# Seven products for the down projection, pair products in one bank, and the up projection's conv in PSUM

## The chip, the cores and the metric

The kernel runs on one core of a Trainium2 chip. The metric is the device time of one execution in microseconds; the time of a kernel is the median of its runs. Beside the timed runs one execution is profiled, and its span (first to last instruction) is a little shorter than its time.

## What is computed

One decoder layer on 1024 tokens of width 1024, all float32. Two mixers and an output projection come first; the change touches only what follows them, the gated feed-forward block:

```python
h = rms_norm(x, norm_ffn_g[i])
u = causal_depthwise_conv(h @ w_up[i], conv_ffn_w[i], conv_ffn_b[i])     # FFN_CONV = 3
u_gate, u_val = jnp.split(u, 2, axis=-1)                                 # D_FF = 2816 columns each
x = x + (jax.nn.silu(u_gate) * u_val) @ w_down[i]
```

## The kernel before

**Matmuls.** Each float32 operand is split into a rounded high part and the low rest (`split`, lines 151 to 154: ScalarE casts, another engine subtracts), and `mm3` (lines 173 to 177) makes one product of three matmuls: high by high, high by low, low by high. Each takes a 128x128 stationary tile and 512 moving columns and adds into one PSUM bank. There are eight banks: two in the pool `pl` (tile `lin`) and six in `psd` (tile `dps`, function `bank6`).

**Up projection.** The 2816 gate columns and as many value columns form 22 column tiles j of 128 each. One tile j covers gate tile j and value tile j for both halves of the tokens: a 2x2 block product, with the contraction of 1024 cut in two. It is made with seven products instead of eight, in the Winograd form of Strassen's method, each of 12 matmuls: p1 and p2 (`p12`), p3 (`22`), p4 (`t4`), p5 (`t1`), p6 (`t2`), p7 (`t3`). The activations' quarters and their sums (`BQ`) stay in SBUF for all j. The weights' sums are made for each j by GpSimd (`w_sums`), and their splits by `w_first`, `w_second` (GpSimd subtracts), `w_third`, `w_fourth` (VectorE subtracts).

Banks of one tile before: x holds p1 and then p1+p6; y holds p2, then p7+p4; z holds p5, then p5+p3. VectorE adds across banks: `c11` = y + a copy of x, `both_sums` q = z + s2 (s2 a copy of x), `c22` = y + q, p3's sum = z + s2, `c21` = y + s2. A matmul that adds to a bank waits until the reads of that bank are done.

`conv` then runs per kind on the whole row of 1024 tokens in an SBUF tile (`uc0`, `uc1`): ScalarE writes bias and last tap, VectorE adds two taps. `gate` applies silu on ScalarE; `value` multiplies on VectorE (line 1368) and stores the row to DRAM (`a_d`, line 1369).

**Order.** TensorE's instructions are chained in program order to the end. From `strict` to `strict_end` (tiles j = 0 and 1 with the activations' quarters made beside them) every engine but SP is chained too. Elsewhere the scheduler places each engine's instructions, earlier lines of the program first where several are ready, so work written later can be placed earlier. Tile j = 2 comes through the strict part with its p1 and p2 done, in two banks of `psd`. The loop `for j in range(3, FFT + 1)` computes tile j - 1 (`q`) while it prepares tile j (`nx`); its product order before is p5, p6, p7, p3, p4, then p12 of the next tile. In its last round `first_acts` loads the first four rows for the down projection.

**Down projection.** For each half of the output columns: eight banks (one for each 128 tokens), eleven pairs of 128-rows kp, each with 2 x 8 products of three matmuls. Weights are split by ScalarE and VectorE (`load_w`), and the rows of `a_d` are loaded and split once for each half. At the end VectorE adds the residual (`xr`) and SP stores.

Of the kernel before, what the change touches and what calls it, by code (L numbers as in the profile page):

```python
# [9 lines left out]
F32 = mybir.dt.float32  # L10
# [7 lines left out]
P = 128  # L18
# [54 lines left out]
def tile_hybrid_layer(ctx: ExitStack, tc: tile.TileContext, x, cols, cons, w_main, w_small, w_uq, w_ukv,  # L73
# [34 lines left out]
    def col(c):  # L108
        return cl[:, c:c + 1]
# [42 lines left out]
    def split(raw, hi, lo, eng=None):  # L152
        S.copy(hi, raw)  # L153
        (eng or V).tensor_sub(lo, raw, hi.bitcast(F32))  # L154
# [8 lines left out]
    def load_w(src, shape):  # L163
        hi = wpool.tile(shape, F32R, name="whi")
        lo = wpool.tile(shape, F32R, name="wlo")
        n = shape[1] // 2
        for j in range(2):
            s = slice(j * n, (j + 1) * n)
            flat = "p a b -> p (a b)"
            load_split(src[:, s, :].rearrange(flat), 512, hi[:, s, :].rearrange(flat), lo[:, s, :].rearrange(flat))  # L170
        return hi, lo

    def mm3(ps, a, b, first, last, **more):
        (ah, al), (bh, bl) = a, b
        PE.matmul(ps, lhsT=ah, rhs=bh, start=first, stop=False, **more)  # L175
        PE.matmul(ps, lhsT=ah, rhs=bl, start=False, stop=False, **more)  # L176
        PE.matmul(ps, lhsT=al, rhs=bh, start=False, stop=last, **more)  # L177
# [979 lines left out]
    def w_third(q):  # L1157
        q.c = w_split(q.r2, w_tiles(2), V)
# [4 lines left out]
    def bank6():  # L1163
        return psd.tile([P, 512], F32, name="dps")
# [5 lines left out]
    with tc.tile_pool(name="ep", bufs=2) as ep:  # L1170
# [117 lines left out]


        tp = tpctx.enter_context(tc.tile_pool(name="tp", bufs=12, side="right"))  # L1290
        a_d = dram.tile([FFT * P, T], F32, name="a_d")
# [19 lines left out]
        def c11(q):  # L1311
            s1 = lt.tile([P, 512], F32, name="lt")
            S.copy(s1, q.x)
            V.tensor_tensor(q.ug[:, 2:514], q.y, s1, op=ALU.add)

        def p5(q):
            q.z = bank6()
            drain([product(q.z, q.b, 0, "t1", True, True)])

        def p6(q, sums=True):  # L1320
            drain([product(q.x, q.b, 4, "t2", False, True)])
            q.s2 = lt.tile([P, 512], F32, name="lt")
            S.copy(q.s2, q.x)
            if sums:
                both_sums(q)

        def both_sums(q):
            q.q = lt.tile([P, 512], F32, name="lt")
            V.tensor_tensor(q.q, q.z, q.s2, op=ALU.add)
# [8 lines left out]

        def c22(q):
            value_row(q)  # L1340
            V.tensor_tensor(q.uv[:, 514:1026], q.y, q.q, op=ALU.add)

        def conv(q, kind, u):
            c = ux[0].tile([P, T], F32, name=f"uc{kind}", bufs=2 - kind)
            ct = kind * FFT + q.j
            cw = CG_FW + 3 * ct
            S.activation(c, u[:, 2:T + 2], AF.Identity, bias=col(CG_FB + ct), scale=col(cw + 2))
            for k in range(2):
                V.scalar_tensor_tensor(c, u[:, k:k + T], col(cw + k), c, op0=ALU.mult, op1=ALU.add)
            return c  # L1350

        def p3(q):
# [1 line left out]
            V.tensor_tensor(q.ug[:, 514:1026], q.z, q.s2, op=ALU.add)  # L1354

        def gate(q):
            q.gate = conv(q, 0, q.ug)
            S.activation(q.gate, q.gate, AF.Silu)

        def p4(q):  # L1360
            drain([product(q.y, q.e or q.c, 0 if q.e else 4, "t4", False, True)])

        def c21(q):
            V.tensor_tensor(q.uv[:, 2:514], q.y, q.s2, op=ALU.add)

        def value(q):
            c = conv(q, 1, q.uv)
            V.tensor_tensor(q.gate, q.gate, c, op=ALU.mult)
            nc.sync.dma_start(out=a_d[q.j * P:(q.j + 1) * P, :], in_=q.gate)

# [52 lines left out]
        low()  # L1423
        flush()
        for q in (q0, q1):
            p5(q)
        def sums(q):

            q.q = q.ug[:, 514:1026]
            V.tensor_tensor(q.q, q.z, q.s2, op=ALU.add)  # L1430
# [6 lines left out]
        p6(q0, False)  # L1437
        sums(q0)
# [3 lines left out]
        p6(q1, False)  # L1442
# [5 lines left out]
        V.tensor_tensor(q0.q, q0.y, q0.q, op=ALU.add)  # L1448
        sums(q1)
        for i in range(2):  # L1450
            job("22", i, b[4, i], act_tile())
        p7(q1)
        V.tensor_tensor(q1.q, q1.y, q1.q, op=ALU.add)
        for i in range(2, 4):
            job("22", i, b[4, i], act_tile())
        low()
# [19 lines left out]
    rows = "p a b -> p (a b)"  # L1476
    first = []

    def first_acts(k):
        raw = up.tile([P, KD, P], F32, name=f"ur{1 + k % 2}", bufs=2).rearrange(rows)  # L1480
        nc.sync.dma_start(out=raw, in_=a_d[k * P:(k + 1) * P, :])
        first.append([tp.tile([P, 2, 512], F32R, name="tq").rearrange(rows) for _ in range(2)])
        split(raw, *first[k])

    for j in range(3, FFT + 1):
        nx = None
        if j < FFT:
            nx = Pair()
            nx.j = j
            w_raw(nx)  # L1490
            w_first(nx)
        p5(q)
        if j == 3:
            gate_row(q)
            c11(q)
# [9 lines left out]
        if nx:  # L1505
            w_second(nx)
        if not nx:
            for k in range(2):
                first_acts(k)
        p7(q)  # L1510
        c22(q)
# [8 lines left out]
        if not nx:  # L1520
            for k in range(2, 4):
                first_acts(k)
        value(q)
        if nx:
            w_third(nx)
            drain([p12(nx)])
            c11(nx)
        q = nx


    upctx.close()

    with tc.tile_pool(name="fp", bufs=6) as fp:
        for ch in range(2):
            banks = [bank6() if t < 6 else lin_tile() for t in range(NT)]
            xrs = []
            for kp in range(FFT // 2):
                wh, wl = load_w(w_down[ch, kp], [P, 2, 512])
                if kp == FFT // 2 - 2:
                    for t in range(NT):  # L1540
                        xrs.append(fp.tile([P, 512], F32, name="xr", bufs=8))
                        nc.sync.dma_start(out=xrs[t], in_=x2_d[t * P:(t + 1) * P, ch * 512:(ch + 1) * 512])
                pair = []
                for k in range(2 * kp, 2 * kp + 2):
                    if ch == 0 and k < 4:
                        pair.append(first[k])
                        continue
                    ar = fp.tile([P, T], F32, name="ar")
                    nc.sync.dma_start(out=ar, in_=a_d[k * P:(k + 1) * P, :])
                    hi = hp.tile([P, T], F32R, name="h")  # L1550
                    lo = hp.tile([P, T], F32R, name="h")
                    split(ar, hi, lo)
                    pair.append((hi, lo))
                last = kp == FFT // 2 - 1
                order = [(k, t) for t in range(NT) for k in range(2)] if last else \
                    [(k, t) for k in range(2) for t in range(NT)]
                for k, t in order:
                    hi, lo = pair[k]
                    tk = slice(t * P, (t + 1) * P)
                    mm3(banks[t], (hi[:, tk], lo[:, tk]), (wh[:, k, :], wl[:, k, :]), kp == 0 and k == 0, last and k == 1)  # L1560
                    if last and k == 1:
                        V.tensor_tensor(xrs[t], banks[t], xrs[t], op=ALU.add)
                        nc.sync.dma_start(out=out[tk, ch * 512:(ch + 1) * 512], in_=xrs[t])
    tpctx.close()
    uctx.close()

# [92 lines left out]
```

## Time and profile before

| what | value |
|---|---|
| median of 3 runs | 2217.35 us (2217.06 to 2220.04) |
| profiled execution, its own time | 2218.69 us |
| its span | 2216.9 us |
| TensorE matmul busy | 2174.5 us (98%), 11104 matmuls recorded |
| VectorE (DVE), ScalarE (ACT), GpSimd (POOL) busy | 1426.3, 1006.5, 818.5 us |
| mean granted TensorE clock | 0.995 |

How to read the rows: "L1141" is line 1141 of the kernel, which may be a helper's. A row of a group reads: line, engine, operation, written tile <- read tiles, shapes, count, then busy time and the mean time of one (ns), then idle time of the engine just before them and what ended it. A row of a timeline reads: start, duration (both us), engine, line, operation, tiles, with the idle time before it in brackets. A row of waits reads: who <- on whom: total us, times, longest. A row of windows gives for each engine its busy time and the instructions that touch the window. Matmuls overlap each other, so their spacing is taken from counts per time, not from the duration of one.

### The profile page before, as it was taken

To read this page: it belongs to the slowest core of one execution; us is meant where nothing else is said; L and a number is where in the kernel's file an instruction comes from. 1 tells how busy PE (TensorE), PEld (TensorE's weight loads), DVE (VectorE), ACT (ScalarE), POOL (GpSimd) and SP (SyncE) were. 2 spreads that over 40 slices of the span, in tenths; PEclk is the share of its full clock that TensorE was granted. 3 is DMA by queue.
4 is the path that set the end of the run, shared out by engine and by line. 5 is a ranking of instruction groups with operands and counts; after the bars stand their busy time and mean duration, and the time that the engine had idled before them with its cause. 6 is when DMAs were issued, how large, how long until landed. Compare 5 with 4: busy or idle time off the path is not lost.

```text
span 2216.9 us, 30483 instructions
## 1 busy us (share of the span) xinstructions
PE 2174.5 (98%) x11104; PEld 1748.1 (79%) x11104; DVE 1426.3 (64%) x2480; ACT 1006.5 (45%) x1820; POOL 818.5 (37%) x911
## 2 busy tenths in 40 slices
PE   8999999999999999999999999999899999999999
PEld 6887777777777887878878788887688888888887
DVE  4566656675664469898786745546977777764432
ACT  5445454544453446666564424335544444443220
POOL 2234433442343247665546210012555555510000
PEclk9999999999999999999999999999899999999999
DMA  4221111101212224645276566542122222246631
GB/s 146 71 65 54 40 48 59 54 32 53 69 43 100 80 86 147 195 143 185 83 240 206 173 223 197 168 159 92 67 95 86 86 76 86 78 143 244 205 127 67
DMA packets 115751, 253.52 MB, mean 114 GB/s; under 512 B 13136, under 2 KB 25360, under 8 KB 115600
## 3 DMA queue, kind: packets, MB, share of 16 engines
q1 hardware_dynamic: 103104, 210.54, 28.5%
q0 software_dynamic: 11008, 37.76, 5.3%
q10 hardware_dynamic: 1488, 3.28, 0.4%
q8 instruction: 87, 1.43, 0.3%
q14 instruction: 64, 0.52, 0.1%
HBM read 194.63 MB, written 56.89 MB: 113 GB/s over the span
## 4 chain that ended last, share of the span: by engine, by line
PE 80%; DVE 9%; DMA 4%; ACT 4%; issue 2%; POOL 1%; SPq 0%; ACTq 0%; DVEq 0%; POOLq 0%
PE lin L175 13%; PE lin L177 13%; PE lin L176 13%; PE dps L176 8%; PE dps L175 8%; PE dps L177 8%; PE pv L670 2%; PE s L175 2%; PE s L176 2%; PE s L177 2%; PE s L627 1%; DMA wraw<-in_w_ssd 1%; PE yp L891 1%; PE sn L874 1%; PE s L610 1%
## 5 line engine op out<-in xcount | busy, mean ns | idle before, releaser
L175 PE MATMUL lin<-h,whi 128*128 128x512 f32 x1440 | 592.2, 411 | 0.3 <-DVE lt L330 0.3
L177 PE MATMUL lin<-h,wlo 128*128 128x512 f32 x1440 | 564.0, 392 | 0.0
L176 PE MATMUL lin<-h,whi 128*128 128x512 f32 x1440 | 562.9, 391 | 0.0
L175 PEld LDWEIGHTS lin<-h,whi 128*128 128x128 f32 x1440 | 271.0, 188 | 82.5 <-issue 33.6
L177 PEld LDWEIGHTS lin<-h,wlo 128*128 128x128 f32 x1440 | 270.8, 188 | 59.9 <-DVE wlo L154 0.2
L176 PEld LDWEIGHTS lin<-h,whi 128*128 128x128 f32 x1440 | 271.9, 189 | 52.9 <-issue 6.7
L153 ACT CAST whi<-wraw 128x512 fp32r<-128x512 f32 x276 | 166.0, 619 | 285.6 <-PE lin L176 115.6
L154 POOL TENSOR_TENSOR wlo<-wraw,whi 128x512 fp32r<-128x512 f32 x134 | 192.5, 1455 | 164.1 <-ACT whi L153 163.9
L664 POOL TENSOR_TENSOR acc<-acc,e 128x512 f32<-128x512 f32 (+3 forms) x80 | 78.7, 984 | 251.1 <-ACT e L659 227.6
L659 ACT ACTIVATE e<-s 128x512 f32<-128x512 f32 (+1 forms) x192 | 93.6, 493 | 169.0 <-DVE s L657 142.9
L154 DVE TENSOR_TENSOR wlo<-wraw,whi 128x512 fp32r<-128x512 f32 x142 | 97.0, 704 | 99.4 <-ACT whi L153 99.2
L154 DVE TENSOR_TENSOR h<-ar,h 128x1024 fp32r<-128x1024 f32 x40 | 48.7, 1225 | 109.2 <-ACT h L153 104.8
L850 ACT ACTIVATE seg<-abc,acum 128x128 f32<-128x128 f32 x256 | 80.2, 390 | 51.0 <-PE yp L891 45.0
L153 ACT CAST h<-ar 128x1024 fp32r<-128x1024 f32 x40 | 42.0, 1054 | 125.4 <-PE lin L176 114.1
L176 PE MATMUL dps<-wlo,h 128*128 128x512 f32 x240 | 93.4, 389 | 0.0
L175 PE MATMUL dps<-whi,h 128*128 128x512 f32 x240 | 93.4, 389 | 0.0
L177 PE MATMUL dps<-whi,h 128*128 128x512 f32 x240 | 93.4, 389 | 0.0
L812 DVE SCALAR_TENSOR_TENSOR xg<-craw,cl,xg 128x1024 f32<-128x1024 f32 x48 | 73.8, 1538 | 27.4 <-ACT xg L810 26.9
L664 DVE TENSOR_TENSOR acc<-acc,e 128x512 f32<-128x512 f32 (+3 forms) x80 | 55.0, 688 | 37.6 <-ACT e L659 37.0
L1140 ACT CAST xhi<-ur 128x512 fp32r<-128x512 f32 (+1 forms) x41 | 34.0, 830 | 90.3 <-PE dps L176 84.2
L670 PE MATMUL pv<-e,vt 128*64 128x512 f32 (+3 forms) x384 | 72.9, 498 | 0.0
L629 DVE CUSTOM_DVE_ANT_0 s<-s,negw 128x128 f32<-128x128 f32 (+3 forms) x128 | 62.3, 495 | 13.6 <-PE s L627 13.5
(587 smaller groups left out, 5045.8 us busy)
## 6 DMA issues: line engine op xcount, KB each, us to landing
wraw<-in_w_main SPq DMA_DIRECT2D x112, 256.0 KB
ur<-in_w_up SPq DMA_DIRECT2D x44, 512.0 KB
ar<-a_d SPq DMA_DIRECT2D x40, 512.0 KB
abc<-ac_d POOLq DMA_DIRECT2D x32, 512.0 KB, 5.2
wraw<-in_w_ssd SPq DMA_DIRECT2D x64, 256.0 KB
wraw<-in_w_down SPq DMA_DIRECT2D x44, 256.0 KB
a_d<-uc SPq DMA_DIRECT2D x22, 512.0 KB
g_d<-lt SPq DMA_DIRECT2D x32, 256.0 KB
```

Source lines behind the costliest of these rows:

```text
L153: S.copy(hi, raw)
L154: (eng or V).tensor_sub(lo, raw, hi.bitcast(F32))
L175: PE.matmul(ps, lhsT=ah, rhs=bh, start=first, stop=False, **more)
L176: PE.matmul(ps, lhsT=ah, rhs=bl, start=False, stop=False, **more)
L177: PE.matmul(ps, lhsT=al, rhs=bh, start=False, stop=last, **more)
L629: V.tensor_tensor_reduce(ps[:, 0:w], ps[:, 0:w], negw[:, 512 - w:512], 1.0, 2 * NEG, ALU.add, ALU.max, nm[:, j, i:i + 1])
L659: S.activation(e[:, c0:512], ps[:, 0:w], AF.Exp)
L664: (V if hd else G).tensor_tensor(accs[hd][:, c0:512], accs[hd][:, c0:512], e[:, c0:512], op=ALU.add)
L670: PE.matmul(pv[hd * 64:(hd + 1) * 64, c0:512], lhsT=vt[:, j, hd * 64:(hd + 1) * 64], rhs=es[hd][:, c0:512], start=first, stop=last)
L812: V.scalar_tensor_tensor(c, raw[:, k:k + T], col(cw + k), c, op0=ALU.mult, op1=ALU.add)
L850: S.activation(seg[:, hd, :], abc[:, hd, :], AF.Relu, bias=acum[:, c, 8 * g + hd:8 * g + hd + 1], scale=-1.0)
L1140: S.copy(hi, r)
```

## The change

Four things are done together.

1. *Down projection.* It becomes a 2x2 block product too: two halves of the tokens by two halves of the output columns, contracted over pairs of 128-rows (even rows, odd rows). Seven products replace eight. They run in four passes over the eleven pairs; the banks `xb` (four) and `yb` (four) collect them, and `evacuate` adds banks to result tiles between passes: pass 1 ends with xb and yb into `r11`, pass 2 with xb into `r12` and yb into `r22`, pass 3 with xb into `r22` and yb into `r12`, pass 4 (one product) with xb into `r21`.
2. *Operands for it.* `value` now makes, for each pair of tiles, the sums of gated quarters on GpSimd (one after the even tile, four after the odd) and stores seven quarters to `f_d`, three from SP and four from GpSimd's queue. The weights' sums are made on GpSimd within passes 2, 3 and 4. `first_operands` loads and splits operands and weights of the first four pairs in the last round.
3. *Pair products in one bank.* p7 and p4 add to x as p6 did, so x holds p1, p1+p6, p1+p6+p7, then p4 on top. `both_sums` goes; ScalarE copies z after p5 instead (q), `c22` = x + q, and `c21` is a ScalarE copy of x. The loop's order becomes p5, p6, p3, p7, p12 of the next tile, p4, and `w_third` follows p4. In the last round p4 has a bank of its own, q.y.
4. *Conv in banks.* `conv` works on half the tokens, with its result in a bank of `psd` (`bank6`) instead of SBUF; gate and value call it twice, and silu and the product read the bank.

```diff
-        def p5(q):
+        def p5(q, z=None):
             q.z = bank6()
             drain([product(q.z, q.b, 0, "t1", True, True)])
+            q.q = lt.tile([P, 512], F32, name="lt") if z is None else z
+            S.copy(q.q, q.z)

-        def p6(q, sums=True):
+        def p6(q):
             drain([product(q.x, q.b, 4, "t2", False, True)])
             q.s2 = lt.tile([P, 512], F32, name="lt")
             S.copy(q.s2, q.x)
-            if sums:
-                both_sums(q)
...
         def p7(q):
-            q.y = bank6()
-            drain([product(q.y, q.c, 0, "t3", True, True)])
+            drain([product(q.x, q.c, 0, "t3", False, True)])
...
-            V.tensor_tensor(q.uv[:, 514:1026], q.y, q.q, op=ALU.add)
+            V.tensor_tensor(q.uv[:, 514:1026], q.x, q.q, op=ALU.add)

-        def conv(q, kind, u):
-            c = ux[0].tile([P, T], F32, name=f"uc{kind}", bufs=2 - kind)
+        def conv(q, kind, u, half):
+            c = bank6()
...
+            n = half * 512
+            S.activation(c, u[:, n + 2:n + 514], AF.Identity, bias=col(CG_FB + ct), scale=col(cw + 2))
             for k in range(2):
-                V.scalar_tensor_tensor(c, u[:, k:k + T], col(cw + k), c, op0=ALU.mult, op1=ALU.add)
+                V.scalar_tensor_tensor(c, u[:, n + k:n + k + 512], col(cw + k), c, op0=ALU.mult, op1=ALU.add)
...
         def gate(q):
+            q.gate = ux[0].tile([P, T], F32, name="uc0", bufs=2)
+            for half in range(2):
+                S.activation(q.gate[:, hs_(half)], conv(q, 0, q.ug, half), AF.Silu)
...
         def c21(q):
-            V.tensor_tensor(q.uv[:, 2:514], q.y, q.s2, op=ALU.add)
+            S.copy(q.uv[:, 2:514], q.x)

         def value(q):
-            c = conv(q, 1, q.uv)
-            V.tensor_tensor(q.gate, q.gate, c, op=ALU.mult)
-            nc.sync.dma_start(out=a_d[q.j * P:(q.j + 1) * P, :], in_=q.gate)
+            for half in range(2):
+                g = q.gate[:, hs_(half)]
+                V.tensor_tensor(g, g, conv(q, 1, q.uv, half), op=ALU.mult)
+            kp = q.j // 2
+            t0, t1 = q.gate[:, 0:512], q.gate[:, 512:1024]
+            def total(n, a, b, op, t):
+                G.tensor_tensor(t, a, b, op=op)
+                if n:
+                    nc.gpsimd.dma_start(out=f_d[kp][:, n, :], in_=t)
+                return t
+            def raw():
+                return wpool.tile([P, 512], F32, name="wraw", bufs=2)
+            if q.j % 2 == 0:
+                nc.sync.dma_start(out=f_d[kp][:, 0, :], in_=t0)
+                even[:] = [t1, total(4, t1, t0, ALU.subtract, ux[0].tile([P, 512], F32, name="ud", bufs=1))]
+            else:
+                nc.sync.dma_start(out=f_d[kp][:, 1:7:5, :], in_=q.gate.rearrange("p (a b) -> p a b", b=512))
+                total(2, even[0], t1, ALU.add, raw())
+                total(3, even[1], t1, ALU.add, raw())
+                t = total(0, t1, t0, ALU.subtract, raw())
+                total(5, t, even[1], ALU.add, t)
```

The loop's new order, and the core of the down projection (pass 1, whose first four pairs come from `first`; pass 2; the end of pass 4):

```diff
         p5(q)
...
         p6(q)
...
         p3(q)
...
         gate(q)
         if nx:
             w_fourth(nx)
-        p4(q)
-        c21(q)
...
+        p7(q)
+        c22(q)
         if nx:
-            w_third(nx)
             drain([p12(nx)])
             c11(nx)
+            p4(q)
+            c21(q)
+            w_third(nx)
...
+        value(q)
...
+        for k in range(nk):
...
+            products(xb, halves(a, 0), bs[0], k == 0, False)
+            if k < 4:
+                others.append((halves(a, 1), bs[1]))
+                if k < 3:
+                    continue
+                for n in range(3):
+                    products(yb, *others[n], n == 0, False)
+            products(yb, halves(a, 1), bs[1], False, k == nk - 1)
+        evacuate(ALU.add, r11, xb, r11)
+        evacuate(ALU.add, r11, yb, r11)
+        stored(0, 0, r11)
+        for k in range(nk):
+            a = acts(k, 2)
+            w = raw_w()
+            nc.sync.dma_start(out=w, in_=w_down[1, k])
+            G.tensor_tensor(w[:, 0, :], kept[:, k, :], w[:, 0, :], op=ALU.subtract)
+            G.tensor_tensor(kept[:, k, :], w[:, 1, :], w[:, 0, :], op=ALU.add)
...
+            products(xb, halves(a, 1), bs[0], False, False)
+            products(yb, halves(a, 0), bs[1], k == 0, False)
+        evacuate(ALU.add, r12, xb, r12)
+        evacuate(ALU.subtract, r22, r22, yb)
...
+        for t in range(4):
+            tk = slice(t * P, (t + 1) * P)
+            for k in range(nk - 3, nk):
+                mm3(xb[t], [v[:, tk] for v in ops[k][0]], ops[k][1], False, k == nk - 1, skip_group_check=True)
+            V.tensor_tensor(r21[:, t, :], xb[t], r21[:, t, :], op=ALU.add)
+            stored(1, 0, r21, slice(t, t + 1))
```

`products` makes four token tiles of 12 matmuls in all (the same `mm3`), `acts` loads 512 KB of `f_d` and splits it, and `raw_w` takes one of four weight buffers. In the strict part q of tiles 0 and 1 is the copy that p5 makes, on ScalarE, and the VectorE sums of z and s2 (line 1430) go.

More of the change, by code (lines that the diff above doesn't have):

```diff
@@ L1290, in tile_hybrid_layer @@
         tp = tpctx.enter_context(tc.tile_pool(name="tp", bufs=12, side="right"))
-        a_d = dram.tile([FFT * P, T], F32, name="a_d")
+        f_d = dram.tile([FFT // 2, P, 7, 512], F32, name="f_d")
+        even = []
         def product(ps, hl, c0, name, first, last):
@@ L1425, in tile_hybrid_layer @@
         for q in (q0, q1):
[L1426 to L1430, printed above, removed]
+            p5(q, q.ug[:, 514:1026])
         for i in range(4):
@@ L1447, in tile_hybrid_layer @@
         p7(q0)
-        V.tensor_tensor(q0.q, q0.y, q0.q, op=ALU.add)
-        sums(q1)
+        V.tensor_tensor(q0.q, q0.x, q0.q, op=ALU.add)
         for i in range(2):
@@ L1452, in tile_hybrid_layer @@
         p7(q1)
[L1453 removed]
+        V.tensor_tensor(q1.q, q1.x, q1.q, op=ALU.add)
         for i in range(2, 4):
@@ L1477, in tile_hybrid_layer, with split_pair, first_operands @@
     first = []
[L1479 to L1483, printed above, removed]
+    def split_pair(raw, tile):
+        hl = [tile().rearrange(rows)[:, 0:raw.shape[1]] for _ in range(2)]
+        split(raw, *hl)
+        return hl
+    def first_operands(k):
+        a, b = [up.tile([P, KD, P], F32, name=f"ur{n}", bufs=2).rearrange(rows) for n in (1, 2)]
+        nc.sync.dma_start(out=a, in_=f_d[k][:, 0:2, :].rearrange(rows))
+        nc.sync.dma_start(out=b, in_=w_down[0, k].rearrange(rows))
+        first.append((split_pair(a, act_tile), split_pair(b, tq)))
     for j in range(3, FFT + 1):
@@ L1504, in tile_hybrid_layer @@
             gate_row(nx)
-        if nx:
             w_second(nx)
-        if not nx:
+        else:
             for k in range(2):
-                first_acts(k)
-        p7(q)
-        c22(q)
+                first_operands(k)
         p3(q)
@@ L1517, in tile_hybrid_layer @@
             w_fourth(nx)
-        p4(q)
-        c21(q)
[L1520 to L1523, printed above, removed]
+        p7(q)
+        c22(q)
         if nx:
-            w_third(nx)
             drain([p12(nx)])
             c11(nx)
+            p4(q)
+            c21(q)
+            w_third(nx)
+        else:
+            q.y = bank6()
+            t = lt.tile([P, 512], F32, name="lt")
+            S.copy(t, q.x)
+            p4(q, q.y)
+            V.tensor_tensor(q.uv[:, 2:514], q.y, t, op=ALU.add)
+            for k in range(2, 4):
+                first_operands(k)
@@ L1528, in tile_hybrid_layer @@
+        value(q)
         q = nx
     upctx.close()
[L1533 to L1563, printed above, removed]
```

95 lines of the change are left out of this document (84 added, 11 removed).

## The prediction

> **What bounds the kernel now.** I read the page first: its span, the busy shares and the chain of work that ended last.
>
> ```profile
> span 2216.9 us, 30483 instructions
> ...
> PE 2174.5 (98%) x11104; PEld 1748.1 (79%) x11104; DVE 1426.3 (64%) x2480; ACT 1006.5 (45%) x1820; POOL 818.5 (37%) x911
> ...
> PE 80%; DVE 9%; DMA 4%; ACT 4%; issue 2%; POOL 1%; SPq 0%; ACTq 0%; DVEq 0%; POOLq 0%
> ```
>
> TensorE is busy 98% of the span and carries 80% of the chain, so matmuls that go should be worth their full spacing wherever the other engines keep up. Next I cut the part that the change touches into stages: the first three column tiles of the up projection (1535 to 1610), its loop (1610 to 1972), the down projection (1972 to 2213) and that stage's heaviest stretch of loads (1990 to 2040); then five single rounds of the loop, of which the mean is quoted. A number with x counts instructions.
>
> ```profile
> core 0: us, PE busy (x) PEld busy (x) DVE busy (x) ACT busy (x) POOL busy (x), PEclk, DMA share, GB/s
> 1535.00:1610.00 75.00, 64.70 (x273) 51.43 (x274) 65.31 (x75) 42.14 (x59) 28.34 (x19) 0.91 0.17 57
> 1610.00:1972.00 362.00, 362.00 (x1580) 296.23 (x1579) 268.18 (x234) 158.07 (x174) 195.65 (x141) 1.00 0.24 86
> 1972.00:2213.00 241.00, 240.81 (x1060) 198.58 (x1058) 90.12 (x102) 65.52 (x83) 0.00 (x0) 1.00 0.49 165
> 1990.00:2040.00 50.00, 50.00 (x222) 41.25 (x221) 20.84 (x22) 19.01 (x23) 0.00 (x0) 1.00 0.77 276
> ...
> sum 96.35, PE 96.35 PEld 78.81 DVE 69.95 ACT 41.15 POOL 55.47; mean PE 19.27 PEld 15.76 DVE 13.99 ACT 8.23 POOL 11.09
> ```
>
> In loop and down projection TensorE never rests. Its spacing is 362.00/1580 = 0.2291 us a matmul in the loop and 241.00/1060 = 0.2274 us below it. The one soft place is the start of the up projection, 64.70 busy of 75.00 at a clock of 0.91. TensorE's waits there:
>
> ```profile
> PE dps L175 <- DVE lt L1329: 6.5, 1, 6.5
> PE dps L175 <- DVE ug L1448: 2.0, 1, 2.0
> ```
>
> **The change part by part.** *Down projection.* Before, 8 token tiles x 22 k x 2 column halves x 3 matmuls = 1056. After, seven products (six groups of 11 x 12 in the first three passes, one in the fourth) = 924. So 132 go, at 0.2274 us: **-30.0 us**, if each pass is fed. Per k of a pass there are 24 matmuls, 5.46 us. What the other engines must do in that time is bounded by these rows (the old down stage's split: L153 and L154 for 1024 columns, L154 for 512):
>
> ```profile
> L154 DVE TENSOR_TENSOR h<-ar,h 128x1024 fp32r<-128x1024 f32 x40 | 48.7, 1225 | 109.2 <-ACT h L153 104.8 <-DMA xr<-x_d 4.2
> L153 ACT CAST h<-ar 128x1024 fp32r<-128x1024 f32 x40 | 42.0, 1054 | 125.4 <-PE lin L176 114.1 <-DMA ar<-a_d 11.2
> L154 DVE TENSOR_TENSOR wlo<-wraw,whi 128x512 fp32r<-128x512 f32 x52 | 35.9, 727 | 27.3 <-ACT whi L153 27.3
> ```
>
> VectorE: 1.225 + 2 x 0.727 = 2.7 us; ScalarE, whose 1024 columns take 1.054: 2 x 1.054 = 2.1 us; both under 5.46. Loads: 512 KB of operand and 512 KB of weight per k, 1.05 MB/5.46 us = 192 GB/s; residual and result, 8.4 MB over 210 us, add 40. The row 1990:2040 carried 276 GB/s at a share of 0.77 with TensorE busy 50.00 of 50.00, so I cost the loads at nothing; if that cover fails, passes stretch to the loads' time.
>
> GpSimd is new here: two sums of 512 in pass 2, one in pass 3. How it and VectorE get on when both work from SBUF shows in the loop:
>
> ```profile
> 1786.62 2.40 POOL L1141 TENSOR_TENSOR wlo<-ur,whi 128x1024 fp32r<-128x1024 f32 x1
> 1789.10 2.15 POOL L1152 TENSOR_TENSOR ur<-ur,us 128x512 f32<-128x512 f32 x1
> ...
> 1795.91 1.30 POOL L1150 TENSOR_TENSOR us<-us,ur 128x512 f32<-128x512 f32 x1
> ...
> 1786.90 3.20 DVE L1368 TENSOR_TENSOR uc<-uc,uc 128x1024 f32<-128x1024 f32 x1
> ...
> 1801.92 1.21 DVE L1141 TENSOR_TENSOR xlo<-ur,xhi 128x1024 fp32r<-128x1024 f32 x1
> ```
>
> VectorE's product L1368 starts at 1786.90, ends at 1790.10, and 1.21 us is what such an operation takes alone: it ran when GpSimd's 2.40 was over, and GpSimd's next took 2.15 where 1.30 is usual. They take turns. In pass 2 the turns sum to 2 x 1.30 + 2.7 = 5.3 us of 5.46. It fits, barely, and the pass starts with operands made in pass 1, where GpSimd rests. I take 0. The Trainium skill's page "SBUF — State Buffer", section "Who interferes with whom", says that a VectorE instruction with two SBUF inputs and a GpSimd one that reads SBUF exclude each other for a whole instruction. By that rule pass 2 has next to no room, which speaks against this change; the rows above agree with it, and the sum is the same by either unless the turns overrun (a rival below).
>
> Between passes VectorE empties four banks (each some 0.69 us, the row of L1329 below) before the next pass writes them: 2.8 us, under the other four banks' last 12 matmuls, 2.73 us, plus at most one split already begun (1.2). I take 0.7 at each of three places, 2 us together with the start (the fifth k's operands fall due 96 matmuls, 21.8 us, after the loop, about when the last pair's stores free the space). **+2**, bounds 0 and +12 (three stops of 4 us).
>
> *Loop.* The matmuls are the same 84 a round, so it stays 19.27 us unless a new wait shows. Terms come from these rows:
>
> ```profile
> L1368 DVE TENSOR_TENSOR uc<-uc,uc 128x1024 f32<-128x1024 f32 x19 | 57.8, 3041 | 0.1
> ...
> L1349 DVE SCALAR_TENSOR_TENSOR uc<-uv,cl,uc 128x1024 f32<-128x1024 f32 x38 | 50.1, 1320 | 0.6
> ...
> L1141 DVE TENSOR_TENSOR xlo<-ur,xhi 128x512 fp32r<-128x512 f32 x18 | 29.4, 1633 | 0.0
> L1140 ACT CAST whi<-us 128x1024 fp32r<-128x1024 f32 x18 | 18.9, 1048 | 81.0 <-PE lin L176 76.2 <-PE lin L177 4.8
> L1329 DVE TENSOR_TENSOR lt<-dps,lt 128x512 f32<-128x512 f32 x19 | 13.1, 691 | 41.2 <-ACT lt L1323 41.2
> L1323 ACT COPY lt<-lin 128x512 f32<-128x512 f32 x19 | 11.0, 581 | 2.4 <-PE lin L177 2.4
> gt<-g_d POOLq DMA_DIRECT2D x16, 256.0 KB, 4.0
> 1440.62 0.54 POOL L1215 DMA_DIRECT2D gt<-g_d  x1 [0.85 <-DVE m L1230]
> ```
>
> VectorE: the conv's four steps of 1.32 become eight of 512 columns with the accumulator in PSUM. Before has no such form: bounds 0.66 (half of 1.32) and 1.32; I take 0.69, the row of a sum that reads a bank. The gate product falls from 3.04 to 2 x 0.69 and two sums go (0.69 each): 13.99 - 1.66 - 1.38 + 0.24 = 11.2 us, 16.2 at the upper bound; hidden under 19.27 either way. ScalarE gains two copies (0.58): 8.23 to some 9.6. GpSimd per pair of rounds: 2 x 11.09 + 5 sums x 1.30 + 4 DMA issues x 0.54 = 30.8 of 38.5; with sums of 2.15 and one wait of 4.0 for a buffer whose store must land, 39.1. Its next weights may start when p6 ends, 5.5 us into the round, and are due at 19.2, with 1.05 + 2.40 of work: 10 us of room. Hidden.
>
> New waits on one bank: p3 waits for ScalarE's copy after p5 (0.58, under p6's 12 x 0.2291 = 2.75); p7 waits for the copy after p6 (behind a cast: 1.05 + 0.58 = 1.63, under p3's 2.75); p4 waits for c22, behind the gate's work on VectorE (0.69 + 4 x 0.69 + 1.63 + 0.69 = 5.8 from p3's end, under p7 and p12, 8.2). SP's queue loses nothing that it waits for. **0**; bounds 0 and +1.5 a round.
>
> *First three tiles.* With both_sums gone, the 6.5 us wait for VectorE at L1329 goes, and with it the half clock behind it (twelve matmuls at 0.43 instead of 0.23):
>
> ```profile
> 1598.92 0.43 PE dps L176
> ...
> 1603.61 0.43 PE dps L175
> ```
>
> That is 8.9 us. But what is late next? Six banks now also hold the conv, and four are still held by q2.x, q2.y, z0 and z1 when tile 0's value conv is ready (ScalarE began it at 1575.19; z1 was read by the sum at 1587.96):
>
> ```profile
> 1575.19 1.24 ACT L1347 ACTIVATE uc<-uv,cl 128x1024 f32<-128x1024 f32 x1
> ...
> 1587.96 0.68 DVE L1354 TENSOR_TENSOR ug<-dps,lt 128x512 f32<-128x512 f32 x1
> ```
>
> If it takes the last two, the gate's halves take z0's and z1's, the latter free near 1588, and p5 of tile 2, which began at 1582, waits some 6 us for a bank: the stop moves rather than goes. I take **-2**, bounds -8.9 and +7. In the written-out order ScalarE's copies of z0 and z1 stand ahead of the t3 casts, which costs VectorE's chain to L1448 about **+0.7** (bounds -1, +3).
>
> Sum: -30.0 + 2 + 0 - 2 + 0.7 = -29.3. The profiled execution took 2218.7 (span 2216.9 and 1.8 around it): 2189.4. The median of the runs shown is 1.3 lower, 2217.35, so **2188 us**.
>
> **Rivals.** (1) *The stop at tile 2 really goes*: VectorE has less to do there, and its conv no longer takes turns with GpSimd. -30.0 + 2 - 8.9 + 0.7: 2181. Against: the bank count. (2) *The passes are not fed*: turns of VectorE and GpSimd overrun in pass 2 (sums at 2.15: 7.0 against 5.46, 11 x 1.5 = 17 us), or stops at the pass changes (12): 2198 to 2205. For: 5.3 of 5.46; against: buffers some four k deep and the idle VectorE before. (3) *Bank starvation each round*: z, y and four conv halves share six banks; 1.5 us x 19 rounds = 28: 2216, no change. Against: each bank is wanted again only a round later. (4) *Slower: GpSimd becomes the loop's bound.* 39.1 a pair, and its four weight differences at 3.31, as an early row shows once, instead of 2.40 add 3.6: 42.7 against 38.5, 4.2 x 10 pairs = 42 us, less 29: 2230. It decides once GpSimd needs over 41.4 a pair. Against: 30.8 by the usual rows, and the change takes VectorE off the common turns.
>
> ```profile
> 1596.39 3.31 POOL L1141 TENSOR_TENSOR wlo<-us,whi 128x1024 fp32r<-128x1024 f32 x1
> ```
>
> **How the numbers follow.** Forecast 0.57, (1) 0.16, (2) 0.18, (3) 0.05, (4) 0.04. The range 2179 to 2204 holds the first two and most of (2). A measurement here tells 0.2%, 4.4 us, from no change: faster holds the forecast, (1), (2) and part of (3), 0.92; same 0.03; slower 0.05.
>
> **What would show it.** Down stage near 212 us with 924 matmuls and TensorE busy throughout; rounds of 19.27 with GpSimd near 15; a wait of p5 for a bank near 1582 in place of L1329's. It is wrong if TensorE waits for GpSimd every second round, for VectorE in pass 2, or if a round is longer than 19.3 us.

## The result, and the profile after

The changed kernel takes 2204.07 us (median of 4 runs, 2203.96 to 2209.94) where the kernel before takes 2217.58; the ratio is 0.9943, with a 95% interval of 0.9931 to 0.9954. It is faster, by 13.5 us. The forecast was 2188, or 29 us less, so about half of the expected gain is missing, and the time lies just above the range.

The page of the changed kernel, the lines that answer to those shown of before:

```profile
span 2202.2 us, 30596 instructions
...
PE 2151.8 (98%) x10972; PEld 1723.4 (78%) x10972; DVE 1446.8 (66%) x2567; ACT 1050.6 (48%) x1938; POOL 971.3 (44%) x1049
```

132 matmuls are gone, as the change says, and the busy share says nothing of what is missing: it is 98% as before. The stages say it. Each stage is cut at the same matmul in both kernels: the first 300 matmuls behind the last transpose, the next 1400 (the loop), the rest of the loop, and the down projection. First before, then after:

```profile
1549.60:1633.00 83.40, 73.97 (x303) 59.23 (x301) 75.09 (x77) 43.11 (x55) 40.79 (x30) 0.92 0.24 82
1633.00:1954.30 321.30, 321.30 (x1402) 262.92 (x1401) 232.57 (x200) 136.03 (x149) 183.20 (x131) 1.00 0.23 82
1954.30:1972.60 18.30, 18.30 (x81) 14.99 (x80) 16.07 (x19) 10.96 (x14) 0.00 (x0) 1.00 0.36 129
1972.60:2212.60 240.00, 240.00 (x1057) 198.07 (x1055) 89.74 (x101) 65.18 (x82) 0.00 (x0) 1.00 0.49 165
```

```profile
1549.30:1628.30 79.00, 70.32 (x303) 55.89 (x301) 62.55 (x83) 47.80 (x74) 45.39 (x41) 1.00 0.26 90
1628.30:1950.10 321.80, 321.80 (x1402) 263.11 (x1401) 216.54 (x255) 163.66 (x235) 245.99 (x209) 1.00 0.30 105
1950.10:1970.30 20.20, 18.63 (x81) 14.95 (x80) 16.51 (x20) 12.51 (x17) 6.33 (x4) 1.00 0.65 205
1970.30:2198.00 227.70, 220.30 (x925) 177.09 (x923) 140.88 (x125) 75.01 (x93) 79.48 (x46) 0.98 0.56 202
```

The first tiles give 4.4 us, the loop takes 0.5 more, its end 1.9 more, and the down projection falls by 12.3, not by 30. Two things make up the 17.7 us between. The first is that TensorE is busy for only 220.30 of 227.70 us: it stops three times, and behind each of these stops some eight matmuls follow at 0.427 us instead of 0.232 (a granted clock of 0.98 in the mean). TensorE's waits from the loop on (the third, L1323, is in the loop's last round; L153 and L154 are one stop):

```profile
PE dps L175 <- DVE xr L1602: 3.3, 1, 3.3
PE dps L175 <- DVE uv L1550: 1.9, 1, 1.9
PE dps L175 <- ACT lt L1323: 1.6, 1, 1.6
PE dps L175 <- ACT tq L153: 1.3, 1, 1.3
PE dps L176 <- DVE tq L154: 0.8, 1, 0.8
```

Summed over the spacings of the matmuls, with what the half clock adds, the stops inside the down projection cost 13.2 us. The second thing is in no row of waits. In the same 40 us of steady work (2100 to 2140), before and after:

```profile
2100.00:2140.00 40.00, 40.00 (x178) 33.15 (x177) 14.09 (x16) 11.53 (x15) 0.00 (x0) 1.00 0.59 190
```

```profile
2100.00:2140.00 40.00, 40.00 (x174) 32.44 (x173) 30.82 (x22) 14.40 (x15) 15.52 (x7) 1.00 0.49 158
```

TensorE is fully busy at a granted clock of 1.00 in both, and makes 174 matmuls where it made 178. From start to start a matmul takes 0.2267 us before and 0.2324 after. Over the 924 that stay this is 5.3 us, or 4.6 against the old stage's own mean of 0.2274, which holds some slower ones.

### The profile page after: what moved, and what is told of

It is laid out like the page before. It is cut to its first block, busy times and chain, and to the rows that moved or that the text cites. A ratio compares the mean times of both kernels' runs of the same rounds, so it can differ in the third digit from the quotient of the medians.

```text
span 2202.2 us, 30596 instructions
## 1 busy us (share of the span) xinstructions
PE 2151.8 (98%) x10972; PEld 1723.4 (78%) x10972; DVE 1446.8 (66%) x2567; ACT 1050.6 (48%) x1938; POOL 971.3 (44%) x1049
## 5 line engine op out<-in xcount | busy, mean ns | idle before, releaser
L154 POOL TENSOR_TENSOR wlo<-wraw,whi 128x512 fp32r<-128x512 f32 x134 | 192.7, 1455 | 164.4 <-ACT whi L153 163.7
L153 ACT CAST whi<-wraw 128x512 fp32r<-128x512 f32 x232 | 141.0, 619 | 258.1 <-PE lin L176 121.0
L1141 DVE TENSOR_TENSOR xlo<-ur,xhi 128x512 fp32r<-128x512 f32 (+1 forms) x41 | 83.2, 2029 | 61.0 <-ACT xhi L1140 61.0
L154 DVE TENSOR_TENSOR wlo<-wraw,whi 128x512 fp32r<-128x512 f32 x98 | 69.8, 722 | 72.1 <-ACT whi L153 71.7
L175 PE MATMUL dps<-tq,h 128*128 128x512 f32 x242 | 97.5, 403 | 6.6 <-DVE xr L1602 3.3
L176 PE MATMUL dps<-tq,h 128*128 128x512 f32 x242 | 97.6, 403 | 0.8 <-DVE tq L154 0.8
L177 PE MATMUL dps<-tq,h 128*128 128x512 f32 x242 | 97.3, 402 | 0.0
L154 DVE TENSOR_TENSOR h<-ar,h 128x1024 fp32r<-128x1024 f32 (+1 forms) x35 | 56.7, 1623 | 24.5 <-ACT h L153 24.3
L1217 POOL DMA_DIRECT2D mt<-m_d x16 | 8.6, 540 | 144.6 <-DVE gt L1226 96.8
L629 DVE CUSTOM_DVE_ANT_0 s<-s,negw 128x128 f32<-128x128 f32 (+3 forms) x128 | 62.3, 495 | 13.5 <-PE s L627 13.4
```

The source lines that it names most:

```text
L629: V.tensor_tensor_reduce(ps[:, 0:w], ps[:, 0:w], negw[:, 512 - w:512], 1.0, 2 * NEG, ALU.add, ALU.max, nm[:, j, i:i + 1])
L1141: eng.tensor_sub(lo, r, hi.bitcast(F32))
```

## Experiments

Each run is compared with the kernel before on the same chip, where that kernel took 2218.8 to 2222.2 us, so times are told as ratios. Stages are read from the profiles, one execution of each run. `last` and `behind` in the edits are helpers of the kernel that place one instruction behind another in the order of its engine.

**The spacing.** In the loop of the kernel before the same two spacings occur, by pairs of operand tiles: whi with h 0.227, whi with tq and xhi with h 0.233. Those pools begin at different places of SBUF. One pad moves every tq tile by 128 bytes:

```diff
+        pad = tpctx.enter_context(tc.tile_pool(name="pad", bufs=1, side="right")).tile([P, 32], F32, name="pad")
+        G.memset(pad, 0.0)
         tp = tpctx.enter_context(tc.tile_pool(name="tp", bufs=12, side="right"))
```

> Only a pad tile of 128 bytes a partition is added, so that every tq tile starts 128 bytes lower in SBUF. In the down stage of the changed kernel every matmul follows the last after 0.2324 us, in the old one after 0.2267, and in the up loop the pairs of operand tiles fall into the same two classes (weights whi with activations h 0.227; whi with tq, and xhi with h, 0.233). Theory A: the spacing depends on where the two operand tiles start relative to each other. Then the down stage falls to about 0.227 and gives back 924 x 0.0055 = 5.1 us; in the up loop whi with tq gets faster (12 matmuls a round) and xhi2 with tq slower (24 a round), some 0.1 us a round slower, so 2 us lost: 2201 +- 2. Rival B: the spacing comes from the passes themselves (banks added to across passes, the loads beside them): spacing stays at 0.232 and the time at 2204.

The ratio is 0.9927 (0.991 to 0.9945). The stretch from 2100 to 2140 again:

```profile
2100.00:2140.00 40.00, 40.00 (x178) 33.10 (x178) 28.09 (x24) 15.44 (x16) 14.39 (x7) 1.00 0.51 164
```

178 matmuls, 0.2267 us each; in the loop xhi with tq went from 0.229 to 0.233, as foreseen. So 128 bytes of an unused tile set the spacing. The down stage fell only from 227.7 to 224.2, since TensorE now reached the stops earlier and waited longer there: the one between passes 1 and 2 ended at 2043.3, where it had ended at 2043.1, and the wait in it grew from 3.3 to 5.7 us.

**The three stops.** At the start of the down projection the fourth bank is q.y, which p4 of the last tile used. ScalarE's and VectorE's rows there:

```profile
1971.55 1.05 ACT L153 CAST tq<-ur 128x1024 fp32r<-128x1024 f32 x1 [0.78 <-DMA ur<-in_w_down]
1972.50 0.58 ACT L1548 COPY lt<-lin 128x512 f32<-128x512 f32 x1
```

```profile
1972.63 1.23 DVE L154 TENSOR_TENSOR tq<-ur,tq 128x1024 fp32r<-128x1024 f32 x1 [0.76 <-ACT tq L153]
1973.77 0.69 DVE L1550 TENSOR_TENSOR uv<-dps,lt 128x512 f32<-128x512 f32 x1
```

VectorE's sum L1550 empties that bank, and it needs ScalarE's copy L1548. On ScalarE a cast that waits for a load stands ahead of the copy, and on VectorE the subtraction that belongs to this cast stands ahead of the sum. The first edit puts the weights' splits behind (its core; inside `first_operands` b's cast goes behind a and its subtraction behind v):

```diff
             S.copy(t, q.x)
+            a = last(mybir.EngineType.Activation)
             p4(q, q.y)
             V.tensor_tensor(q.uv[:, 2:514], q.y, t, op=ALU.add)
+            v = last(mybir.EngineType.DVE)
             for k in range(2, 4):
-                first_operands(k)
+                first_operands(k, (a, v))
```

> The weights' splits of the third and fourth pair in the last round are put behind ScalarE's copy of x and VectorE's sum that empties q.y. Theory A: the stop of 2.1 us at the start of the down projection (TensorE on the sum of q.y) comes from these splits, which stood ahead on both engines and waited for a load; it falls below 0.5 us and the half-clock stretch behind it (8 matmuls at 0.43) goes too: 3 to 4 us less, 2200.5. Rival B: the fourth bank is late for another reason (six banks are too few here): the stop stays, 2204.

0.9926 (0.9911 to 0.9941), with a down stage of 226.7. The stop is gone, but the next one grew from a spacing of 1.68 to one of 4.37: little is won. That second stop ends with operands of the fifth pair. What held them:

```profile
1986.02 1.30 POOL L1375 TENSOR_TENSOR wraw<-wraw,ud 128x512 f32<-128x512 f32 x1
```

```profile
1987.35 1.82 SPq L1608 DMA_DIRECT2D kept<-in_w_down  x4
1989.21 0.49 SPq L1588 DMA_DIRECT2D ar<-f_d  x1
```

```profile
1996.22 1.04 ACT L153 CAST h<-ar 128x1024 fp32r<-128x1024 f32 x1 [20.25 <-DMA ar<-f_d]
```

SP issues no load into the new tiles before GpSimd's last sum has ended, at 1987.32: that sum reads a tile of the pool whose storage kept and ar take over. The second edit lets VectorE make the sums of the last pair:

```diff
-                G.tensor_tensor(t, a, b, op=op)
+                (V if q.j == FFT - 1 else G).tensor_tensor(t, a, b, op=op)
...
-                t = total(0, t1, t0, ALU.subtract, raw())
+                t = lt.tile([P, 512], F32, name="lt") if q.j == FFT - 1 else raw()
+                t = total(0, t1, t0, ALU.subtract, t)
```

> The last pair's four sums are made by VectorE instead of GpSimd. Theory A: the stop at the fifth pair (1.45 + 1.1 us, and half clock behind it, 4.5 us in all) comes from loads of kept and ar that cannot be issued before the last GpSimd sum has read the up stage's tiles (issue at 1987.35, the sum's end at 1987.3); with VectorE the sums end about 4 us earlier, the loads start by 1983.5 and the stop goes or shrinks below 0.7: 2200 +- 1. Rival B: the loads themselves are too slow (DMA): they start earlier but the stop stays within 1 us of what it was, 2203 to 2204.

0.9921 (0.9903 to 0.9938). The loads start 12.2 us after the down projection's first matmul instead of 17.0, the stop at the fifth pair is gone, and the down stage falls to 223.6. The third stop is at the change from pass 1 to pass 2:

```profile
2036.70 1.77 DVE L154 TENSOR_TENSOR tq<-kept,tq 128x512 fp32r<-128x512 f32 x1
2038.40 2.32 DVE L154 TENSOR_TENSOR h<-ar,h 128x1024 fp32r<-128x1024 f32 x1
2040.64 1.75 DVE L154 TENSOR_TENSOR tq<-kept,tq 128x512 fp32r<-128x512 f32 x1
2042.32 2.47 DVE L1602 TENSOR_TENSOR xr<-dps,xr 128x512 f32<-128x512 f32 x4
```

```profile
2037.89 1.75 POOL L1639 TENSOR_TENSOR whi<-kept,whi 128x512 f32<-128x512 f32 x1
2039.71 2.13 POOL L1640 TENSOR_TENSOR kept<-whi 128x512 f32<-128x512 f32 x1
```

The sums that empty the banks (L1602) stand behind splits for pass 2, and these take 1.75 and 2.32 us where 0.68 and 1.21 are usual, because GpSimd makes pass 2's sums at the same time. Third edit (pass 2, k > 1):

```diff
+        out_of_banks = last(mybir.EngineType.DVE)
         stored(0, 0, r11)
         for k in range(nk):
             a = acts(k, 2)
+            if k > 1:
+                behind(out_of_banks)
...
                 split(v, h_, l_)
+                if k > 1:
+                    behind(out_of_banks)
```

> In pass 2 VectorE's splits from the third pair on are put behind the sums that empty the banks after pass 1. Theory A: the stop of 3.5 us between passes 1 and 2 (5.2 with the half clock behind it) comes from four splits that stood ahead of those sums on VectorE, each 1.8 to 2.3 us instead of 0.7 to 1.2 because GpSimd's sums were taking turns with them; with the order changed the stop falls below 1 us: 2199.5 +- 1. Rival B: without the early splits the operands of the third and fourth pair come late, and a stop of similar length appears some 10 us later: 2203 to 2205.

0.9916 (0.9897 to 0.9935), down stage 221.9; that stop is gone and none comes in its place behind it. The other two stops moved as well in this profile (spacings of 0.6 instead of 2.3 and of 4.2 instead of 1.7), so not all of the 5.8 us belong to this edit. In time the medians of these four runs lie within 2.4 us of each other, and their intervals overlap with that of the changed kernel (0.9931 to 0.9954): the profiles show what each edit does, the times don't. The three edits of order together:

> The changed kernel with the three edits of order together: the weights' splits behind the emptying of q.y, the last pair's sums on VectorE, pass 2's splits behind the emptying of the banks. Theory A (the three stops are three causes): the down stage loses its 13.2 us of stops and half clock but for 1 to 2, falls from 227.8 to 216 at a spacing still of 0.232, and the time to 0.987 to 0.990 of before (2189 to 2194 where before takes 2217). Rival B (taking one stop away moves the wait to the next load, as the first edit alone did): the down stage stays over 221, 0.991 or more.

0.9903 (0.9888 to 0.9917). The down stage:

```profile
1971.30:2187.40 216.10, 215.55 (x926) 173.82 (x924) 138.29 (x131) 75.70 (x94) 75.41 (x42) 1.00 0.58 213
```

TensorE is busy 215.55 of 216.10: of 13.2 us, 1.4 are left. Each of the three stops went with its own edit. Alone the edits took 1.0, 4.1 and 5.8 us off the down stage, together 11.6, and only together are they clear of the changed kernel in time. Last, with the pad for tq and longer rows ug and uv, all operand tiles of loop and down projection start at the same place of a 256 byte step:

```diff
-            q.ug = up.tile([P, T + 2], F32, name="ug", bufs=2)
+            q.ug = up.tile([P, T + 64], F32, name="ug", bufs=2)
...
-            q.uv = ux[0].tile([P, T + 2], F32, name="uv", bufs=2)
+            q.uv = ux[0].tile([P, T + 64], F32, name="uv", bufs=2)
```

> As the one with the three edits of order, and all operand tiles start at the same place of a 256 byte step: the pad of 128 bytes ahead of tq, and the rows ug and uv 64 elements longer than 1024 instead of 2, which shifts the weight tiles xhi and xlo. Theory A (the spacing depends on where the two operands start): every matmul of the up loop and the down stage at 0.227: rounds 84 x 0.2268 = 19.05 instead of 19.3, 5 us over the loop, and the down stage 924 x 0.2267 + 1 to 2 = 211 us, 5 less: 0.982 to 0.986 of before. Rival B (128 bytes was right for tq and whi by chance, and the weight tiles of the ux pool are slow for another reason): rounds stay at 19.2 to 19.3, only the down stage gains, 0.985 to 0.988.

0.9856 (0.984 to 0.9871), a median of 2186.98. The loop's 1400 matmuls and the down projection:

```profile
1625.20:1942.50 317.30, 317.30 (x1401) 262.83 (x1400) 217.39 (x255) 163.66 (x235) 245.36 (x209) 1.00 0.31 107
1965.50:2176.00 210.50, 210.28 (x926) 173.40 (x924) 134.79 (x129) 75.75 (x94) 76.76 (x42) 1.00 0.60 217
```

Every pair of tiles in both is now at 0.227. The same pad and rows on the kernel before:

> The kernel before with nothing but the equal starts of operand tiles (the pad of 128 bytes, the rows ug and uv 64 elements longer than 1024). Theory A (the spacing is set by where the two operand tiles start, whatever else the kernel does): the 1400 matmuls of the loop take 317.4 us instead of 321.2, every pair of tiles at 0.227; with the first two tiles and the down stage's first 96 matmuls (0.233) some 4.5 to 5.5 us in all, 0.9975 to 0.998 of before. Rival B (the gain needs the changed kernel's banks and order): within 1 us of before, 0.9995 to 1.0005.

0.9981 (0.9971 to 0.9991), and 317.4 us for the 1400 matmuls: so the effect does not need the change.

**The parts alone.** The conv put back into SBUF tiles (the lines of the diff under `conv`, `gate` and `value` undone):

> The changed kernel with the conv back in SBUF tiles over the whole row, all else as changed. Theory A (the conv in banks matters at the start of the up projection and at the two ends of the bank's life, not in the rounds): rounds stay at 19.3 us; the stops of the first three tiles, 8.9 us of waits in the changed kernel, change by 2 to 5 us either way; the stop of 2.1 us for q.y's bank at the start of the down projection goes, since six banks are then enough; in all 2203 to 2208. Rival B (the conv in banks is what keeps VectorE and GpSimd from taking turns, now that GpSimd also makes the quarters' sums): rounds get longer than 19.5, 4 us or more over the loop, and the time passes 2210.

The ratio is 1.0018 (1.0008 to 1.0027): the changed kernel without the conv in banks is slower than before, and the loop's 1400 matmuls take 329.9 us instead of 321.8. The rounds are not all of it: the first 300 matmuls take 87.1 us instead of 79.0, and the loop's end takes some 4.5 us more. Then the down projection's products and their sums alone, on the up projection as it was (the new `f_d`, `value`'s sums, `first_operands` and the four passes in the kernel before):

> The kernel before with the seven products of the down projection and the sums for them alone; pair products and conv in SBUF as before. Theory A (GpSimd's sums need VectorE off the turns, as the run with the conv back in SBUF showed: rounds 0.47 us longer, 8 us over the loop): the loop from the 300th to the 1700th matmul takes 325 to 330 us instead of 321.2, the down stage 224 to 228 instead of 240, together 0.996 to 1.000 of before. Rival B (it was the one bank for the pair's products, with its wait for VectorE at p4, that made those rounds longer): the loop stays within 2 us of 321, 0.993 to 0.9955.

1.0082 (1.0067 to 1.0097), slower by 18 us although the down stage falls to 222.7, and 351.2 us for the loop's 1400 matmuls, more than either theory had. Four rounds of the loop (1700.00 to 1777.20) in before, after, with the conv in SBUF, and with the down projection alone:

```profile
1700.00:1777.20 77.20, 77.20 (x338) 63.17 (x338) 56.46 (x48) 32.95 (x37) 44.14 (x33) 1.00 0.24 82
```

```profile
1700.00:1777.20 77.20, 77.20 (x337) 63.14 (x336) 51.84 (x60) 38.74 (x56) 58.07 (x48) 1.00 0.29 100
```

```profile
1700.00:1777.20 77.20, 75.62 (x325) 60.59 (x325) 59.80 (x39) 33.34 (x42) 68.79 (x49) 1.00 0.29 103
```

```profile
1700.00:1777.20 77.20, 72.98 (x309) 58.56 (x309) 62.77 (x47) 31.01 (x34) 68.25 (x47) 0.98 0.27 96
```

GpSimd's busy time in the same stretch is 58 with the conv in banks and 68 to 69 without. The conv's step, a weight difference and a sum of GpSimd in the rounds (1640 to 1940) say why; after, then with the conv in SBUF:

```profile
L1349 DVE SCALAR_TENSOR_TENSOR dps<-uv,cl,dps 128x512 f32<-128x512 f32 x63 | 42.9, 745 | 0.1
...
L1141 POOL TENSOR_TENSOR wlo<-us,whi 128x1024 fp32r<-128x1024 f32 x15 | 36.2, 2416 | 0.3
...
L1150 POOL TENSOR_TENSOR us<-us,ur 128x512 f32<-128x512 f32 x16 | 20.7, 1296 | 0.6
```

```profile
L1347 DVE SCALAR_TENSOR_TENSOR uc<-uv,cl,uc 128x1024 f32<-128x1024 f32 x31 | 63.8, 2057 | 4.6 <-ACT uc L1345 4.1
...
L1141 POOL TENSOR_TENSOR wlo<-us,whi 128x1024 fp32r<-128x1024 f32 x15 | 48.7, 3248 | 0.1
...
L1150 POOL TENSOR_TENSOR us<-us,ur 128x512 f32<-128x512 f32 x15 | 29.3, 1951 | 0.8
```

With the conv in SBUF its step over 1024 columns takes 2.06 us, where it took 1.28 in the kernel before; there nearly all of these steps ran while GpSimd had no sum or difference under way. GpSimd's sum L1150, which now overlaps the conv, grows from 1.30 to 1.95 us. The difference L1141 grows from 2.42 to 3.25; what runs beside it is not the conv's step but VectorE's subtractions and its product of two rows in SBUF. In the changed kernel 45 of the conv's half steps in these rounds had no GpSimd sum or difference beside them and 33 ran wholly beside one, and all of them took 0.74 to 0.76 us. With the down projection alone TensorE waits for VectorE in nearly every round:

```profile
PE dps L175 <- DVE lt L1330: 24.7, 16, 4.0
```

The Trainium skill's page "SBUF — State Buffer", section "Who interferes with whom", says that a VectorE instruction with two SBUF inputs contends with a GpSimd one that reads SBUF, and that one with at most one SBUF input, outside the modes that use two ports, doesn't. These rows agree with both halves. The two changes of the up projection alone:

> The kernel before with the two changes of the up projection alone (pair products in one bank, conv in banks); the down projection and the store of rows as before. Theory A: the up projection's changes are worth 2 to 4 us, all of it in the first three tiles (83.4 us before, 79.0 after, for the 300 matmuls that follow the last transpose), the rounds and the down stage stay at 19.3 and 240: 0.9980 to 0.9992 of before. Rival B: they are worth nothing by themselves (the gain at the start is given back at the end of the loop, where two waits of 2 us are new in the changed kernel): 0.9995 to 1.0005.

1.0019 (1.0009 to 1.003), neither theory. The first 300 matmuls take 80.0 (83.4 before) as foreseen, but the old down projection wants all eight banks in its first matmuls, and some are still with the conv: it waits 3.2 us for VectorE's last product and 0.5 for silu, half clock follows, and its stage takes 246.1 instead of 240.0. So neither part gains alone. The conv in banks keeps VectorE out of the way of GpSimd's new sums, and the new down projection, whose first products go to four banks, does not wait for the conv's banks in the changed kernel, as the old one does.

**Two more orders**, on top of the kernel with all edits so far. In the last round ScalarE's casts of the first operands wait for loads ahead of its copy of z; all splits of the first four pairs were put behind the copy after p6 (`behind` on each):

> As the kernel with all edits of order and equal starts, and in the last round the splits of the first four pairs are put behind ScalarE's copy of x after p6. Theory A: the stop of 2.0 to 3.8 us in the last round (p3 on ScalarE's copy of z) comes from ScalarE's casts that wait for loads ahead of that copy; it goes, the stretch from the 1700th matmul to the loop's end falls from 20.0 to 23.0 to about 18, and the time by 2 to 5 us, to 0.983 to 0.985 of before. Rival B: the splits, now later, are late for the down projection: a stop of like length appears within its first 10 us.

The loop's end fell from 23.0 to 17.9 us, and a wait of 2.8 us for silu's bank came up some 4 us into the down projection, whose stage grew from 210.5 to 214.1: 0.985 (0.9832 to 0.9867), the same time as without. On top of that, ScalarE's copy of tile 2's first product was put ahead of tile 0's gate:

> As the one before, and ScalarE's copy of tile 2's first product is written ahead of tile 0's gate. Theory A: the stop of 3.4 us at p6 of tile 2 goes, and part of it comes back at p4 of tile 2, which waits for VectorE (2.3 us now): 0 to 2 us less than the run before in the first 300 matmuls. Rival B: VectorE's backlog sets both, and the whole 3.4 us come back behind: no change within 0.5.

0.9862 (0.9843 to 0.9881). TensorE's wait of 3.2 us for that copy, at p6 of tile 2, went, and its wait for VectorE at p4 grew from 2.2 to 5.7 us, with twelve matmuls at 0.427 us behind it: the first 300 matmuls take 81.8 us instead of 78.3. That fits a backlog of VectorE that sets the end of both waits; no run shortened that backlog.

## Why the prediction was wrong

- **Down projection, -30.0.** The count was right, 924 matmuls. The spacing was taken from the old down stage (0.2274) and held not to change; it measured 0.2324. That is 924 x 0.005 = 4.6 us of the missing gain. The rows before showed a spacing of 0.2291 in the loop, which was quoted, put beside 0.2274, and not asked about; split by operand pairs it holds both values.
- **Between the passes and at the start, +2, bounds 0 and +12.** This is the step that failed most: 13.2 us. The cover named for it, that VectorE empties four banks under the other four's last matmuls plus one split already begun, supposed the wanted order on VectorE; when xb's last matmul was done, one split had begun and three more stood ahead of the sums, each stretched by GpSimd (TensorE's wait of 3.3 us, 5.2 with the half clock). The fifth pair's operands were foreseen to fall due about when the last stores free the space; they came some 2 us late (waits of 1.3 and 0.8). And the bank of p4 was not counted at all.
- **Turns of VectorE and GpSimd.** Rival (2) had the mechanism, and in its first form the wrong place: pass 2 did keep up (no stop inside it), the harm was done ahead of the pass change. The prediction had GpSimd rest in pass 1; in the profile it makes pass 2's sums from 2016.14 on, while pass 1's last matmul starts at 2039.4. Rival (2)'s 2198 to 2205 holds the measured time partly by luck, since the one pass change that stopped TensorE is worth 5.2 of the missing 17.7 us. The loads were no limit: 213 GB/s in the run with all edits of order, TensorE busy 215.55 of 216.10.
- **Loop, 0.** Right in sum (+0.5 over 1400 matmuls), and so are GpSimd's 30.8 us a pair (58.07/2 = 29.0) and ScalarE's 9.6 a round (38.74/4 = 9.7). VectorE has 13.0 a round, not 11.2: half of the conv takes 0.75, and w_third's subtraction is stretched. That the conv in banks takes VectorE off the turns was named as what spoke against rival (4). It is more than that: without it the loop gets longer by 8 us, and with the old banks as well by 30. The engine that TensorE waits for with the old banks is VectorE (24.7 us at L1330), kept from its turns, and not GpSimd itself as rival (4) had it. The loop's end was no term at all, and cost 1.9.
- **First three tiles, -2 and +0.7.** Measured -4.4. The stop at L1329 and its half clock went, as said; what came in its place was not a bank for p5 near 1582 (no stop there) but ScalarE's copy of tile 2's first product, 3.1 us, with p4 waiting 2.0. The +0.7 did not show: the wait of 2.0 us at L1448 is 2.0 after as well (L1465). So the gain is larger than forecast, and the stop that is left is another than the one that was priced.

With the three orders and the pads the kernel takes 2187 us. That this is near the forecast is in part luck, for 4 of its 32 us come from a faster loop, which the forecast had at nothing; but the stops and the spacing of the down projection could be had back.

## What to carry to other kernels

When products are taken away from a stage that TensorE bounds, list every bank and every tile whose last reader belongs to the stage before, and who stands ahead of that reader on its engine: the gain is lost in such places. When two engines slow each other, price them together: here two changes that each make the kernel slower alone make it faster together, because one keeps VectorE off the SBUF reads that GpSimd's new sums need. And divide a stage's time by its matmuls, per pair of operand tiles, before taking a spacing from another stage.

## What the runs showed of the hardware

The time from one matmul to the next depends on where in SBUF the operand tiles start. When all of them start at the same place of a 256 byte step, every pair takes 0.2267 us. When the two tiles of a pair are 64 bytes (xhi with h) or 128 bytes apart (tq with whi, tq with h; places from the built programs), it takes 0.232 to 0.234. Nothing waits in the profile, and busy shares and clock are the same. One pair shows that the distance within it is not the whole rule: xhi with tq starts at the same place of the step in the kernels before and after, but not at the place of h, and there a product of twelve matmuls takes 0.227 to 0.2275 us each when it follows one of whi with h, and up to 0.231 when it follows one of xhi with h. Why it is so, and whether the step is 256 bytes, stays open; other distances were not tried.

After a stop the clock was halved in some cases and not in others: after the stop of the changed kernel that ended at 1974.51, 1.9 us long, eight matmuls ran at half rate, and after the one that ended at 1588.17, 3.1 us long, none did. So a stop's price is not read from its length alone.
